# Hybrid decoder layer on one core: a written order for ScalarE and VectorE from the last head's output on, and a last row whose scaling is shared

## The chip, the cores and the metric

One Trainium2 chip, one core of it. The metric is the device time of one execution in microseconds (us); less is better. TensorE is called PE in the profile, VectorE DVE, ScalarE ACT, GpSimd POOL, and SyncE, which issues most transfers, SP.

## The reference

`x` is 1024 tokens by 1024 channels, float32, depth 1:

```python
h = rms_norm(x, norm_mix_g);  u = h @ w_in            # 1024 x 3328: pool 256 | q, f, i, g of 768 each
y_pool = pool_mixer(u_pool, pool_w, pool_scale)       # 4 groups of 64: trailing means over 2/4/8/16, minus the token, a 64x64 map
y_hgrn = hgrn2_mixer(q, f, i, g, lb, norm_g)          # 6 heads, state 128x128: S_t = f_t S_(t-1) + (1-f_t) i_t^T, o_t = S_t^T q_t,
                                                      # then o * rsqrt(mean(o^2)+eps) * norm_g * silu(g) for each head
x = x + concat(y_pool, y_hgrn) @ w_out
x = x + square(relu(rms_norm(x, norm_mlp_g) @ w_up)) @ w_down
return rms_norm(x, final_norm_g)
```

## The kernel before, in words

All products run in float32 made of two parts: `split` (L118 to L122) makes `hi`, a rounded copy by ACT (L121), and `lo`, the rest, by DVE (L122), and `mm3` (L124 to L129) makes one product of three matmuls, hi x hi, hi x lo, lo x hi (128x128 by 128x512 each). So every operand of a product passes through ACT first and DVE second.

The six recurrent heads come one after another. `hgrn(hd)` is a generator that stops before each of its stages ("near", "middle", "far", "keys", "updates", "output"), and between the stages the loop over heads draws steps of other work from `beside(hd)`: the projections of the next head, and beside the last head (hd = 5) the gate of head 4, the second pool input, and the gate of head 5. The table `LAGS` says how many steps are drawn ahead of each stage. In that loop the order of PE alone is written (`tc.manual_schedule(engines={PE})`); the instructions of ACT, DVE and POOL are placed by a scheduler, which may move an instruction ahead of others. Each engine then runs its own list strictly in that order.

Around the last head's output these matter:

- pool input 1 (`pool_input`, L550 on): u (L355), running sums `winK`, `winF` (L565, L566), two closing steps of 1.3 us (L572), then a split into `whi_win` and `wlo_win`, from which PE makes `psp` (`pool_output`), and ACT scales `psp` into `mix[1]` (L589).
- gate of head 5 (`gated`): for each half, ps_g times rms_row to g (L355, DVE), sigmoid of g into ps_g (L361, ACT), product into g (L362, DVE).
- stage "output" of head 5: PE makes `po` (L513, L515) in two banks; ACT squares each of its 8 blocks with a sum (L518); DVE makes the mean (L134, `ms_o`), POOL the power -1/2 (L136, `rstd_o`), DVE scales into `on` (L520). `mixed` transposes `on` on PE (`pto`, L542) and multiplies by the gate into the eighth block of the mixing output (L544).
- the output product: `w_out`'s left half is loaded in four pieces of two row blocks (`wo_1`, `wo_2`, `wo_3`, `wo_0`) into two raw buffers, so that the third load waits until the first piece is split; `mix_split(h, j)` splits block j of the mixing output into `mT`, half h of the tokens. PE takes the blocks in the order 2, 3, 4, 5, 6, 0, 1, 7. For the first two row tiles (`ps_o_0`, `ps_o_1`) it makes blocks 2, 3, 4, then `pto`, then the other five. After them come the row tiles from `ps_o_2` on.

At the very end (from L1134) the down projection's results are added to x row tile by row tile, each row's square sum is made by ACT (L1128), its mean by DVE (L1141), the power by POOL (L1143); the left 512 columns are scaled by DVE (L1147) and sent by SP (L1148), the right 512, already multiplied by the weight, are scaled by ACT (L1151) and sent from ACT's queue (L1152). The last row tile's last product is made in two pieces of 256 columns. Here DVE, ACT and POOL have a written order already.

Of the kernel before, what the change touches and what calls it, by code (L numbers as in the profile page):

```python
# [10 lines left out]
F32 = mybir.dt.float32  # L11
F32R = mybir.dt.float32r
# [20 lines left out]
STAGES = ("near", "middle", "far", "keys", "updates", "output")  # L33
LAGS = {48: (5, 14, 8, 4, 1, 9), 64: (6, 19, 10, 4, 1, 10), 96: (6, 19, 10, 5, 2, 14)}
LAGS = {steps: dict(zip(STAGES, lags)) for steps, lags in LAGS.items()}
# [30 lines left out]
def kernel(  # L66
# [116 lines left out]
    with ExitStack() as pa:  # L183
# [209 lines left out]
        def hgrn(hd, q, f, k, vt):  # L393
# [114 lines left out]
            on = ha.tile([P, NT, P], F32, tag="Kn", name=f"on_{hd}", bufs=1)  # L508
            for b in range(2):
                po = misc_ps(f"po_{hd}_{b}")  # L510
                for c in range(4):
                    i = 4 * b + c
                    pe.matmul(po[:, c * P:(c + 1) * P], sc[:, i, :], vt[:, i, :], start=True, stop=i == 0)  # L513
                    if i:
                        pe.matmul(po[:, c * P:(c + 1) * P], q[:, i * P:(i + 1) * P], st[:, i, :], start=False, stop=True)  # L515
                ss = small.tile([P, 4], F32, tag="sso", name=f"sso_{hd}_{b}")
                for c in range(4):
                    act.activation(junk[:, :P], po[:, c * P:(c + 1) * P], AF.Square, accum_out=ss[:, c:c + 1])  # L518
# [35 lines left out]
        def pool_input(kt, wins):  # L554
            u = ha.tile([P, S], F32, tag="GQ"[kt], name=f"u_{kt}", bufs=1 + kt)
            w = col_tile(kt * P, f"pool{kt}")

            ready_w["g"] = gate_weights(NH - 2 + kt)
# [17 lines left out]
            parts = [wring["split"][0].tile([P, S], F32R, tag=f"w{part}", name=f"w{part}_win_{kt}") for part in ("hi", "lo")]  # L576
# [163 lines left out]
        def row_block(src, r0, n, c0, name):  # L740
            return load_w(src[r0 * P:(r0 + n) * P, c0:c0 + 512].rearrange("(j p) c -> p j c", p=P), [n, 512], name)

        ws = [None] * (KT // 2)
        for j in MIX_ORDER[:-1:2]:
            ws[j // 2] = row_block(w_out[0], j // 2 * 2, 2, 0, f"wo_0_{j // 2}")
        mT = big_pair("mT")

        def mix_split(h, j):
            split(mT[h][0][:, j, :], mT[h][1][:, j, :], mix[j][:, h * 512:(h + 1) * 512])

        for pool_ in (psm, pss, psd):
            pool_.release()
        psb = ctx.enter_context(tc.tile_pool(name="psb", bufs=8, space=bass.MemoryType.PSUM, reuse_waits="tile"))

        def bank(name):
            return psb.tile([P, 512], F32, tag="bank", name=name)

        def products_out(banks, weight, js):

            for j in js:  # L760
                for i, ps in banks.items():
                    m, c = mT[i // 4], i % 4 * P
                    mm3(ps, (m[0][:, j, c:c + P], m[1][:, j, c:c + P]), weight(j), j == MIX_ORDER[0], j == MIX_ORDER[-1])

        def left_weight(j):
            hi, lo = ws[j // 2]
            return hi[:, j % 2, :], lo[:, j % 2, :]


        with tc.manual_schedule(engines={mybir.EngineType.PE}):  # L770
# [7 lines left out]
        for j in MIX_ORDER:  # L778
            mix_split(1, j)
# [338 lines left out]
    with ExitStack() as pd:  # L1118
# [30 lines left out]

        def right_rows(i, r):  # L1150
            act.mul(ys[i][:, 512:], ys[i][:, 512:], r)  # L1151
            act.dma_start(out[0, i * P:(i + 1) * P, 512:], ys[i][:, 512:])  # L1152
# [86 lines left out]
        with tc.manual_schedule(engines={mybir.EngineType.DVE, mybir.EngineType.Activation, mybir.EngineType.Pool}):  # L1239
# [3 lines left out]
            for (g, n), (pools, a, b) in zip(products[-2:], ((pools, a, b), ahead)):  # L1243
                for i, cs in product(g, n, a, b):
                    if cs.stop == 256:

                        ss = squares(i, cs)
                        left_rows(*ready)
# [3 lines left out]
                        continue  # L1252
                    ss = squares(i, cs)
                    if ready:
                        if cs.start % 512 == 0:
# [3 lines left out]
            left_rows(*ready)  # L1259
            right_rows(*ready)  # L1260
# [54 lines left out]
```

## Time and profile before

| | |
|---|---|
| time before, median of 3 runs | 1071.73 us (1071.65 to 1073.27) |
| the profiled execution's own time | 1071.58 us |
| its span, first to last instruction | 1069.8 us |
| PE busy | 1060.4 us (99%) |
| DVE busy | 741.7 us (69%) |
| ACT busy | 447.7 us (42%) |
| POOL busy | 77.3 us (7%) |
| granted clock of PE | 0.999 |

The time is 1.78 us more than the span, which lies around it. In a row of the timeline the first number is the start, the second the duration, both in us; "xN" merges N instructions of one form that follow each other; the bracket says how long the engine sat idle before, and on whom it waited. Instructions of one engine overlap a little, so that the next one starts some 0.06 to 0.1 us before the row of the one before it ends.

### The profile page before, as it was taken

What the parts mean: (1) busy time and instruction counts of PE and PEld (TensorE: products, weight loads), DVE (VectorE), ACT (ScalarE), POOL (GpSimd) and SP (SyncE); (2) the same over time, 40 slices, a digit from 0 to 9 for tenths busy, and PEclk for the clock granted to TensorE, in tenths of its full rate; (3) what the DMA queues carried; (4) which work ended last, traced back from release to release, by engine and by line L of the source; (5) the groups of instructions that cost most, each with busy time, mean ns of one, the idle gap of its engine ahead of it and who ended that gap; (6) DMA issues with size and microseconds to landing.
All of it is one profiled execution on the core that took longest, in us unless ns stands there. A gap on an engine that the chain in (4) does not pass through costs nothing.

```text
span 1069.8 us, 14595 instructions
## 1 busy us (share of the span) xinstructions
PE 1060.4 (99%) x5930; PEld 889.6 (83%) x5930; DVE 741.7 (69%) x928; ACT 447.7 (42%) x722; POOL 77.3 (7%) x126
## 2 busy tenths in 40 slices
PE   9999999999999999999999999999999999999997
PEld 8988889988888788888888888888888888888886
DVE  5377676166587924798856865876979878777775
ACT  5856545344444723463223223323435242423334
POOL 0001000001010111101101100100100000000001
PEclk9999999999999999999999999999999999999999
DMA  9521011031001633135435534428983344253104
GB/s 315 169 60 55 17 30 40 3 97 41 21 1 41 202 134 117 70 108 177 167 109 189 185 101 156 177 98 318 389 335 119 114 162 170 105 204 150 40 1 157
DMA packets 70515, 137.56 MB, mean 129 GB/s; under 512 B 5040, under 2 KB 44080, under 8 KB 66864
## 3 DMA queue, kind: packets, MB, share of 16 engines
q1 hardware_dynamic: 59808, 100.98, 27.8%
q0 software_dynamic: 9344, 33.56, 8.0%
q10 hardware_dynamic: 1296, 2.10, 0.5%
q8 instruction: 46, 0.75, 0.3%
q14 instruction: 21, 0.17, 0.1%
HBM read 98.87 MB, written 37.75 MB: 128 GB/s over the span
## 4 chain that ended last, share of the span: by engine, by line
PE 95%; DVE 3%; DMA 0%; issue 0%; POOL 0%; ACT 0%; SPq 0%; ACTq 0%; POOLq 0%
PE ps_ua L128 5%; PE ps_ua L127 5%; PE ps_ua L129 5%; PE ps_dx L129 5%; PE ps_dx L127 5%; PE ps_dx L128 5%; PE ps_v L283 3%; PE ps_dy L129 3%; PE ps_uc L128 3%; PE ps_dy L127 3%; PE ps_uc L127 3%; PE ps_uc L129 3%; PE ps_dy L128 3%; PE ps_o L129 2%; PE ps_o L128 2%; PE ps_o L127 2%
## 5 line engine op out<-in xcount | busy, mean ns | idle before, releaser
L121 ACT CAST wdop<-raw_wd 128x2048 fp32r<-128x2048 f32 x28 | 53.5, 1912 | 154.3 <-PE ps_dy L129 50.2
L127 PE MATMUL ps_ua<-h2op,whi_wu 128*128 128x512 f32 x256 | 99.7, 389 | 0.0
L129 PE MATMUL ps_ua<-h2op,wlo_wu 128*128 128x512 f32 x256 | 99.6, 389 | 0.0
L128 PE MATMUL ps_ua<-h2op,whi_wu 128*128 128x512 f32 x256 | 99.6, 389 | 0.0
L127 PE MATMUL ps_dx<-wdop,hop 128*128 128x512 f32 x252 | 98.0, 389 | 0.0
L128 PE MATMUL ps_dx<-wdop,hop 128*128 128x512 f32 x252 | 98.0, 389 | 0.0
L129 PE MATMUL ps_dx<-wdop,hop 128*128 128x512 f32 x252 | 98.0, 389 | 0.0
L122 DVE TENSOR_TENSOR wdop<-raw_wd,wdop 128x2048 fp32r<-128x2048 f32 x28 | 64.1, 2289 | 27.9 <-ACT wdop L121 27.9
L121 ACT CAST hop<-hraw 128x2048 fp32r<-128x2048 f32 x28 | 53.4, 1909 | 33.6 <-DMA hraw<-hid 21.0
L122 DVE TENSOR_TENSOR hop<-hraw,hop 128x2048 fp32r<-128x2048 f32 x28 | 63.9, 2283 | 2.2 <-ACT hop L121 2.2
L121 ACT CAST whi_wu<-wsum 128x1024 fp32r<-128x1024 f32 x22 | 23.2, 1053 | 93.6 <-DVE wsum L795 38.7
L122 DVE TENSOR_TENSOR wlo_wu<-raw_wu,whi_wu 128x1024 fp32r<-128x1024 f32 x23 | 28.0, 1221 | 47.6 <-ACT whi_wu L121 47.6
L798 DVE TENSOR_TENSOR x<-ps_dx,x 128x512 f32<-128x512 f32 x64 | 43.9, 687 | 18.7 <-PE ps_dx L129 18.7
L127 PEld LDWEIGHTS ps_ua<-h2op,whi_wu 128*128 128x128 f32 x256 | 48.1, 188 | 10.0
L129 PEld LDWEIGHTS ps_ua<-h2op,wlo_wu 128*128 128x128 f32 x256 | 48.0, 188 | 10.0
L128 PEld LDWEIGHTS ps_ua<-h2op,whi_wu 128*128 128x128 f32 x256 | 48.1, 188 | 9.9
L128 PEld LDWEIGHTS ps_dx<-wdop,hop 128*128 128x128 f32 x252 | 47.3, 188 | 9.9
L129 PEld LDWEIGHTS ps_dx<-wdop,hop 128*128 128x128 f32 x252 | 47.3, 188 | 9.8
L127 PEld LDWEIGHTS ps_dx<-wdop,hop 128*128 128x128 f32 x252 | 47.3, 188 | 9.8
L1031 POOL DMA_DIRECT2D hid<-hid x56 | 29.8, 532 | 283.6 <-DVE hid L1028 216.5
L127 PE MATMUL ps_uc<-h2op,whi_wu 128*128 128x512 f32 x128 | 49.8, 389 | 0.0
L128 PE MATMUL ps_uc<-h2op,whi_wu 128*128 128x512 f32 x128 | 49.8, 389 | 0.0
(280 smaller groups left out, 2706.4 us busy)
## 6 DMA issues: line engine op xcount, KB each, us to landing
hid<-hid POOLq DMA_DIRECT2D x56, 512.0 KB, 3.2
hraw<-hid SPq DMA_DIRECT2D x28, 1024.0 KB, 4.8
raw_wu<-in_w_up_dram SPq DMA_DIRECT2D x32, 512.0 KB, 3.8
raw_wd<-in_w_down_dram SPq DMA_DIRECT2D x16, 1024.0 KB, 7.1
xt<-in_x_t_dram SPq DMA_DIRECT2D x16, 256.0 KB, 5.4
xn<-in_x_dram SPq DMA_DIRECT2D x8, 512.0 KB, 7.9
x<-x_mid SPq DMA_DIRECT2D x8, 512.0 KB, 5.4
raw_q<-in_w_in_dram SPq DMA_DIRECT2D x6, 512.0 KB, 3.9
```

What stands on the lines that cost most here:

```text
L121: act.copy(hi, src)
L122: dve.tensor_tensor(out=lo, in0=src, in1=hi.bitcast(F32), op=ALU.subtract)
L127: pe.matmul(ps, lh, rh, start=start, stop=False, skip_group_check=goes_on)
L128: pe.matmul(ps, lh, rl, start=False, stop=False, skip_group_check=goes_on)
L129: pe.matmul(ps, ll, rh, start=False, stop=stop, skip_group_check=goes_on)
L283: pe.matmul(banks[i][:, :VC], hT[h][part][:, j, i * P:(i + 1) * P], w[:, b, :], start=j == 0 and part == 0 and w is wh, stop=j == KT - 1 a ...
L798: dve.tensor_tensor(out=out_, in0=a, in1=b, op=ALU.add)
L1031: nc.gpsimd.dma_start(store[n][:, at, :], t)
```

## The change

It has two parts.

At the last head: a stage "rows" is put into `hgrn` between the squares and the scaling of `on` (its lag is 0, so that nothing is drawn there). Once head 5 reaches "output", ACT and DVE follow the written order too, through the whole output product's first rows, which now stand within the same region as the loop over heads. In that order stand: the work beside the head, then both banks' squares and means; at "rows" the first piece of w_out (`wo_1`), the splits of blocks 2, 3, 4 and `wo_2`; then the scaling of `on`, the rest of the gate, and, by twos, `wo_3`, blocks 5 and 6, `wo_0`, blocks 0 and 1, `mixed`, block 7, and last the second half's splits. The two tiles of the pool windows' split are taken from their ring before the gate's weights. PE's order stays as it was.

At the end: of the last row tile all four parts of x are multiplied by the weight ahead (`weighted`), DVE makes the last square sum itself, and the scaling is cut at column 704: DVE the left 704, sent by SP, ACT the right 320, sent from ACT's queue (`last_rows`). The row tile before it is finished by ACT one step earlier.

```diff
@@ hgrn @@
             yield "output"
-            on = ha.tile([P, NT, P], F32, tag="Kn", name=f"on_{hd}", bufs=1)
+            pos = []
             for b in range(2):
...
                 for c in range(4):
                     act.activation(junk[:, :P], po[:, c * P:(c + 1) * P], AF.Square, accum_out=ss[:, c:c + 1])
-                r = rstd_of(ss, 4, P, small, f"o_{hd}_{b}")
+                pos.append((po, rstd_of(ss, 4, P, small, f"o_{hd}_{b}")))
+            yield "rows"
+            on = ha.tile([P, NT, P], F32, tag="Kn", name=f"on_{hd}", bufs=1)
+            for b, (po, r) in enumerate(pos):
                 dve.tensor_tensor(
@@ the loop over heads @@
-        with tc.manual_schedule(engines={mybir.EngineType.PE}):
+        def left_rows_of(j):
+            src = w_out[0][j * P:(j + 2) * P, :512].rearrange("(j p) c -> p j c", p=P)
+            ws[j // 2] = load_w(src, [2, 512], f"wo_0_{j // 2}")
...
+        with ExitStack() as in_order:
+            in_order.enter_context(tc.manual_schedule(engines={mybir.EngineType.PE}))
...
                 while stage:
+                    if hd == NH - 1 and stage == "output":
+                        in_order.enter_context(
+                            tc.manual_schedule(engines={mybir.EngineType.DVE, mybir.EngineType.Activation})
+                        )
...
+                    if hd == NH - 1 and stage == "rows":
+                        mix_operand(0)
+                        left_rows_of(MIX_ORDER[0])
+                        for j in MIX_ORDER[:3]:
+                            mix_split(0, j)
+                        left_rows_of(MIX_ORDER[2])
...
-            for j in MIX_ORDER[:-1]:
+            products_out(first_rows, left_weight, MIX_ORDER[:3])
+            left_rows_of(MIX_ORDER[4])
+            for j in MIX_ORDER[3:5]:
                 mix_split(0, j)
-            products_out(first_rows, left_weight, MIX_ORDER[:3])
+            left_rows_of(MIX_ORDER[5])
+            for j in MIX_ORDER[5:7]:
+                mix_split(0, j)
             mixed(NH - 1, on, gates[NH - 1], bank)
             mix_split(0, MIX_ORDER[-1])
             products_out(first_rows, left_weight, MIX_ORDER[3:])
@@ the end @@
+        def last_rows(i, r):
+            y, n = ys[i], 704
+            dve.tensor_scalar(y[:, :n], y[:, :n], r, None, op0=ALU.mult)
+            nc.sync.dma_start(out[0, i * P:(i + 1) * P, :n], y[:, :n])
+            act.mul(y[:, n:], y[:, n:], r)
+            act.dma_start(out[0, i * P:(i + 1) * P, n:], y[:, n:])
+
+        def weighted(i, cs):
+            dve.tensor_tensor(out=ys[i][:, cs], in0=xs[i][:, cs], in1=gf[:, cs], op=ALU.mult)
...
                         ss = squares(i, cs)
+                        weighted(i, cs)
                         left_rows(*ready)
...
+                    if cs.start == 256:
+                        ss = small.tile([P, 1], F32, tag="ss3", name=f"ss3_{i}_last", bufs=16)
+                        x_ = xs[i][:, cs]
+                        dve.scalar_tensor_tensor(
+                            out=junk[:, cs], in0=x_, scalar=1.0, in1=x_, op0=ALU.mult, op1=ALU.mult, accum_out=ss
+                        )
+                        r = row_scale(i, ss)
+                        weighted(i, cs)
+                        right_rows(*ready)
+                        last_rows(i, r)
+                        continue
...
-            left_rows(*ready)
-            right_rows(*ready)
```

ACT's list at the last head's output, before: `mT_hi` from mix_1227, mix_1675, mix_2286, mix_2750, mix_3206, mix_3170 are the casts of blocks 2, 3, 4, 5, 6 and 0, `po` and `sso` the squares, `whi_win` the cast of the pool windows, `ps_g` the gate's sigmoid, `wo` the pieces of w_out.

```order
L121 CAST mT_hi_3533<-mix_1227 128x512
L121 CAST mT_hi_3533<-mix_1675 128x512
L121 CAST mT_hi_3533<-mix_2286 128x512
L121 CAST mT_hi_3533<-mix_2750 128x512
L121 CAST mT_hi_3533<-mix_3206 128x512
L518 ACTIVATE junk,sso_0_3442<-po_0_3434 128x128
L121 CAST mT_hi_3533<-mix_3170 128x512
L121 CAST whi_win_3394<-winK_3066 128x512 x2
L361 ACTIVATE ps_g_0_3401<-g_3400 128x512
L518 ACTIVATE junk,sso_0_3442<-po_0_3434 128x128
L121 CAST whi_wo_1_3511<-raw_wo_1_3509 128x1024
L518 ACTIVATE junk,sso_0_3442<-po_0_3434 128x128
```

The same place on ACT after the change, from the pool windows' cast on, which now follows straight on the copies of `kn`:

```order
L121 CAST whi_win_3190<-winK_3066 128x512 x2
L361 ACTIVATE ps_g_0_3403<-g_3402 128x512
L518 ACTIVATE junk,sso_0_3443<-po_0_3435 128x128 x4
L518 ACTIVATE junk,sso_1_3461<-po_1_3452 128x128 x4
L121 CAST whi_wo_1_3474<-raw_wo_1_3472 128x1024
L121 CAST mT_hi_3470<-mix_1227 128x512
L121 CAST mT_hi_3470<-mix_1675 128x512
L121 CAST mT_hi_3470<-mix_2286 128x512
L121 CAST whi_wo_2_3486<-raw_wo_2_3484 128x1024
```

Six casts of `mT_hi` that stood ahead of the pool windows' cast now stand behind it, behind the sigmoid and behind all eight squares, which stand in one row.

DVE's list from the gate's first half on, before (`lo` parts of the same names; `ms_o`, `on` of head 5's output):

```order
L355 TENSOR_TENSOR g_3400<-ps_g_0_3401,rms_row 128x512
L122 TENSOR_TENSOR wlo_win_3395<-winK_3066,whi_win_3394 128x512 x2
L362 TENSOR_TENSOR g_3400<-ps_g_0_3401,g_3400 128x512
L122 TENSOR_TENSOR mT_lo_3534<-mix_1227,mT_hi_3533 128x512
L122 TENSOR_TENSOR wlo_wo_1_3512<-raw_wo_1_3509,whi_wo_1_3511 128x1024
L122 TENSOR_TENSOR wlo_wo_2_3518<-raw_wo_2_3515,whi_wo_2_3517 128x1024
L134 TENSOR_SCALAR ms_o_0_3447<-sso_0_3442 128x4
```

And after:

```order
L122 TENSOR_TENSOR wlo_win_3191<-winK_3066,whi_win_3190 128x512 x2
L355 TENSOR_TENSOR g_3402<-ps_g_0_3403,rms_row 128x512
L362 TENSOR_TENSOR g_3402<-ps_g_0_3403,g_3402 128x512
L134 TENSOR_SCALAR ms_o_0_3448<-sso_0_3443 128x4
L134 TENSOR_SCALAR ms_o_1_3466<-sso_1_3461 128x4
L122 TENSOR_TENSOR wlo_wo_1_3475<-raw_wo_1_3472,whi_wo_1_3474 128x1024
L122 TENSOR_TENSOR mT_lo_3471<-mix_1227,mT_hi_3470 128x512
L122 TENSOR_TENSOR mT_lo_3471<-mix_1675,mT_hi_3470 128x512
L122 TENSOR_TENSOR mT_lo_3471<-mix_2286,mT_hi_3470 128x512
L122 TENSOR_TENSOR wlo_wo_2_3487<-raw_wo_2_3484,whi_wo_2_3486 128x1024
L523 TENSOR_TENSOR on_3490<-po_0_3435,rstd_o_0_3450 128x512
L523 TENSOR_TENSOR on_3490<-po_1_3452,rstd_o_1_3468 128x512
```

The first lo part of w_out stands behind both means now, and the gate's first product behind the pool windows' lo part. Behind these rows DVE's list goes on with the gate's second half, `wo_3`, blocks 5 and 6, `wo_0`, blocks 0 and 1, where before the gate's second half stood among the scalings of `on`.

DVE's list at the very end, before and after (x_6409 is the last row tile, x_6407 the one before it):

```order
L798 TENSOR_TENSOR x_6409<-ps_last_8270,x_6409 128x256
L1147 SCALAR_TENSOR_TENSOR y<-x_6407,rstd_n_6_8268,gf 128x512
L1250 TENSOR_SCALAR ss_left<-ss_7_0_8284,ss_8092 128x1
L798 TENSOR_TENSOR x_6409<-ps_last_8290,x_6409 128x256
L1141 TENSOR_SCALAR ms_n_7_8308<-ss_7_256_8304,ss_left 128x1
L1147 SCALAR_TENSOR_TENSOR y<-x_6409,rstd_n_7_8310,gf 128x512
```

```order
L819 TENSOR_TENSOR x_6409<-ps_last_8270,x_6409 128x256
L1180 TENSOR_TENSOR y<-x_6409,gf 128x256
L1168 SCALAR_TENSOR_TENSOR y<-x_6407,rstd_n_6_8268,gf 128x512
L1283 TENSOR_SCALAR ss_left<-ss_7_0_8284,ss_8092 128x1
L819 TENSOR_TENSOR x_6409<-ps_last_8291,x_6409 128x256
L1290 SCALAR_TENSOR_TENSOR junk,ss_7_last<-x_6409 128x256
L1162 TENSOR_SCALAR ms_n_7_8307<-ss_7_last,ss_left 128x1
L1180 TENSOR_TENSOR y<-x_6409,gf 128x256
L1174 TENSOR_SCALAR y<-y,rstd_n_7_8309 128x704
```

Two multiplications by the weight and one square sum come to DVE; ACT loses that square sum.

More of the change, by code (lines that the diff above doesn't have):

```diff
@@ L30 @@
 FILL = 160
-STAGES = ("near", "middle", "far", "keys", "updates", "output")
+STAGES = ("near", "middle", "far", "keys", "updates", "output", "rows")
 LAGS = {48: (5, 14, 8, 4, 1, 9), 64: (6, 19, 10, 4, 1, 10), 96: (6, 19, 10, 5, 2, 14)}
-LAGS = {steps: dict(zip(STAGES, lags)) for steps, lags in LAGS.items()}
+LAGS = {steps: dict(zip(STAGES, (*lags, 0))) for steps, lags in LAGS.items()}
 FIRST_LAG = 9
@@ L556, in pool_input @@
             w = col_tile(kt * P, f"pool{kt}")
+            parts = [wring["split"][0].tile([P, S], F32R, tag=f"w{part}", name=f"w{part}_win_{kt}") for part in ("hi", "lo")]
             ready_w["g"] = gate_weights(NH - 2 + kt)
@@ L575, in pool_input @@
                 )
-            parts = [wring["split"][0].tile([P, S], F32R, tag=f"w{part}", name=f"w{part}_win_{kt}") for part in ("hi", "lo")]
             for h in range(2):
@@ L720, with mix_operand, mix_split @@
             split(*(w[pr, :, pr] for w in pws), pw[pr])
-        with tc.manual_schedule(engines={mybir.EngineType.PE}):
+        ws, mT = [None] * (KT // 2), []
+        def left_rows_of(j):
+            src = w_out[0][j * P:(j + 2) * P, :512].rearrange("(j p) c -> p j c", p=P)
+            ws[j // 2] = load_w(src, [2, 512], f"wo_0_{j // 2}")
+        def mix_operand(h):
+            mT.append(tuple(big.tile([P, KT, 512], F32R, tag="big", name=f"mT_{part}{h}") for part in ("hi", "lo")))
+        def mix_split(h, j):
+            split(mT[h][0][:, j, :], mT[h][1][:, j, :], mix[j][:, h * 512:(h + 1) * 512])
+        with ExitStack() as in_order:
+            in_order.enter_context(tc.manual_schedule(engines={mybir.EngineType.PE}))
             for hd in range(NH):
@@ L738 @@
                 finish(work)
[L740 to L767, printed above, removed]
@@ L770, with bank, products_out @@
-        with tc.manual_schedule(engines={mybir.EngineType.PE}):
+            for pool_ in (psm, pss, psd):
+                pool_.release()
+            psb = ctx.enter_context(tc.tile_pool(name="psb", bufs=8, space=bass.MemoryType.PSUM, reuse_waits="tile"))
+            def bank(name):
+                return psb.tile([P, 512], F32, tag="bank", name=name)
+            def products_out(banks, weight, js):
+                for j in js:
+                    for i, ps in banks.items():
+                        m, c = mT[i // 4], i % 4 * P
+                        mm3(ps, (m[0][:, j, c:c + P], m[1][:, j, c:c + P]), weight(j), j == MIX_ORDER[0], j == MIX_ORDER[-1])
@@ L771, with left_weight @@
+            def left_weight(j):
+                hi, lo = ws[j // 2]
+                return hi[:, j % 2, :], lo[:, j % 2, :]
             first_rows = {i: bank(f"ps_o_0_{i}") for i in range(2)}
-            for j in MIX_ORDER[:-1]:
+            products_out(first_rows, left_weight, MIX_ORDER[:3])
+            left_rows_of(MIX_ORDER[4])
+            for j in MIX_ORDER[3:5]:
                 mix_split(0, j)
-            products_out(first_rows, left_weight, MIX_ORDER[:3])
+            left_rows_of(MIX_ORDER[5])
@@ L777 @@
             products_out(first_rows, left_weight, MIX_ORDER[3:])
-        for j in MIX_ORDER:
-            mix_split(1, j)
+            mix_operand(1)
+            for j in MIX_ORDER:
+                mix_split(1, j)
     mixp.release()
@@ L1252 @@
                         continue
+                    if cs.start == 256:
[9 more added lines that the diff above has]
+                        continue
                     ss = squares(i, cs)
                     if ready:
-                        if cs.start % 512 == 0:
-                            left_rows(*ready)
+                        left_rows(*ready)
                         right_rows(*ready)
                     ready = i, row_scale(i, ss)
-            left_rows(*ready)
-            right_rows(*ready)
 _INS = [
```

## The prediction

> **What bounds the kernel now.** I read the page first, then PE's waits, then the timeline of ACT, DVE and PE around the last head's output, and last the end of the span.
>
> ```profile
> span 1069.8 us, 14595 instructions
> PE 1060.4 (99%) x5930; PEld 889.6 (83%) x5930; DVE 741.7 (69%) x928; ACT 447.7 (42%) x722; POOL 77.3 (7%) x126
> ```
>
> PE is busy for all but 9.4 us of the span, and most of those lie behind its last matmul. So a microsecond that PE loses anywhere is a microsecond of the time; nothing later can absorb it. The view of PE's waits has two rows:
>
> ```profile
> PE warm L230 <- DVE junk L228: 1.2, 1, 1.2
> PE ps_o L129 <- DVE mT_lo L122: 0.9, 2, 0.5
> ```
>
> The first is the opening. The second is all that the first part of the change can win: two waits, 0.9 us together, in the first rows of the output product. PE takes the first of those products, and is through with the two row tiles, here (the row at 369.48 is the first product of ps_o_2):
>
> ```profile
> 356.10 0.39 PE L127 MATMUL ps_o<-whi_wo,mT_hi 128*128 128x512 f32 x1
> ...
> 360.18 0.38 PE L542 MATMUL pto<-ident,on 128*128 128x128 f32 x2
> ...
> 369.25 0.39 PE L129 MATMUL ps_o<-whi_wo,mT_lo 128*128 128x512 f32 x1
> 369.48 0.40 PE L127 MATMUL ps_o<-whi_wo,mT_hi 128*128 128x512 f32 x1
> ```
>
> A product starts 0.23 us after the one before it. What PE finds ready at 356.10 depends on ACT and DVE in the ten microseconds before:
>
> ```profile
> 345.78 2.70 ACT L121 CAST mT_hi<-mix 128x512 fp32r<-128x512 f32 x5 [6.87 <-PE ps_g L128]
> ...
> 349.15 1.13 ACT L121 CAST whi_win<-winK 128x512 fp32r<-128x512 f32 x2
> 350.20 0.59 ACT L361 ACTIVATE ps_g<-g 128x512 f32<-128x512 f32 x1
> ```
>
> ```profile
> 347.63 1.28 DVE L572 SCALAR_TENSOR_TENSOR winK<-winF,pconst,u 64x1024 f32<-64x1024 f32 x1
> 348.95 0.35 DVE L504 SCALAR_TENSOR_TENSOR st<-st,dec,pu 128x128 f32<-128x128 f32 x1
> 349.21 0.69 DVE L355 TENSOR_TENSOR g<-ps_g,rms_row 128x512 f32<-128x512 f32 x1
> 349.81 1.28 DVE L122 TENSOR_TENSOR wlo_win<-winK,whi_win 128x512 fp32r<-128x512 f32 x2
> ...
> 352.21 2.36 DVE L122 TENSOR_TENSOR wlo_wo<-raw_wo,whi_wo 128x1024 fp32r<-128x1024 f32 x2
> ```
>
> ACT sat idle for 6.87 us, and the scheduler put five casts of `mT_hi` (2.70 us) there, while the pool windows were not yet done; both pieces of w_out were split by 354.6. That hoist hides what PE needs at 356.10.
>
> **The change part by part: the written order.** ACT now has the pool windows' cast directly behind the copies of `kn`. It waits there for the DVE step that starts at 347.63 in the row above. This step moves by two small edits of about 0.1 us each (one copy more behind `u`, an order of two steps); I take 347.8, end 349.1. Until then ACT stands still with the casts queued behind. From there the two lists give a chain in which each link waits for the one before:
>
> - Two casts of the windows (1.13): 349.1 to 350.25; the first half is there at 349.7, and DVE makes `wlo_win` (1.28) from 349.75 to 351.05. PE wants it at about 352 for `psp`, as before: no cost.
> - DVE now makes the gate's first product (0.69) only behind that, to 351.65, not in the gap at 349.21. The sigmoid (0.59) runs from 351.7 to 352.3.
> - Then the eight squares. Standing in a row they look as at an earlier head:
>
> ```profile
> 303.67 0.28 ACT L518 ACTIVATE junk<-po 128x128 bf16<-128x128 f32 x1
> 303.84 0.19 ACT L518 ACTIVATION_READ_ACCUMULATOR junk<-po 128x1 f32 x1
> 304.07 0.28 ACT L518 ACTIVATE junk<-po 128x128 bf16<-128x128 f32 x1
> ```
>
> - One square starts 0.40 after the one before it, so eight take 3.2 us: 352.2 to 355.4. Before, other work stood between them.
> - ACT casts `wo_1`, 1.05 by the row below: 355.4 to 356.5. Block 2's cast follows, 0.6 (five took 2.70): 357.0. DVE is held at the second mean until 355.5, then by `wo_1`'s cast. It makes `wlo_wo_1` from 356.53 to 357.7 and block 2's lo part to 358.3 (0.69).
>
> So PE's first product waits from 356.1 to 357.0, the second to 357.7, the third to 358.3: waits of 0.9, 0.5 and 0.4, 1.8 in all, where before there was none. From 356.53 DVE is the link without a gap: 1.13 for `wlo_wo_1` (two take 2.36), 3 x 0.60 for blocks 2, 3, 4 (five take 3.10 in the row below), 1.13 for `wlo_wo_2`, 2 x 0.60 for `on` and 0.69 for the gate's second half make 5.95: 362.5. The sigmoid (0.55) and the cast of `wo_3` (1.05 and handing over, 1.1) follow on ACT to 364.15, and DVE makes `wlo_wo_3` (1.13) and block 5's lo part (0.69): 365.97. The third product of block 5 waits for that.
>
> ```profile
> 357.28 1.05 ACT L121 CAST whi_wo<-raw_wo 128x1024 fp32r<-128x1024 f32 x1 [0.27 <-DMA raw_wo<-in_w_out_dram]
> ```
>
> ```profile
> 362.77 3.10 DVE L122 TENSOR_TENSOR mT_lo<-mix,mT_hi 128x512 fp32r<-128x512 f32 x5
> ```
>
> Block 5's products come on PE behind those of blocks 2, 3, 4 and `pto`. Its cast stands on ACT behind `wo_3`'s, which PE does not need before block 6: the written order makes block 5 wait for the wrong thing. PE, 18 products and the 1.0 us of `pto` behind its start, would be there at 363: it waits 1.6 for block 5's cast (364.6) and 0.9 for the lo part. Behind this wait it has 28 products up to ps_o_2 (1 and 3 of block 5, 6 each of blocks 6, 0, 1, 7): 28 x 0.23 = 6.44, from 366.03 to 372.47. Blocks 6, 0, 1 and 7 are ready at least 0.4 before PE wants them in this count. Before, ps_o_2 began at 369.48. **Loss: 3.0 us**, with the 0.9 of waits that disappear counted in. Its ends: 2.0 if a square costs no more than its own row, 0.28, since other work stood between them before; 3.5 if the windows come 0.3 later and a handing over costs 0.2 more.
>
> SP's transfers: `wo_3` may be fetched only once `wo_1`'s lo part is made, 357.7 now. The issue stood at 353.46 and the data at 357.28 (above), 3.8 later:
>
> ```profile
> 353.46 1.50 SPq L164 DMA_DIRECT2D raw_wo<-in_w_out_dram  x2
> ```
>
> So it lands at 361.5, wanted at 363.05: 1.5 to spare. `wo_0` is asked for at 360.7, lands at 364.5, and is wanted at 365.1: hidden, by 0.6. The loads of x and of w_up behind them in SP's queue go 3 us later too, as do their users. The other heads only get a few exchanged rows on DVE, where PE never waits. The second half's splits end near 376; PE wants them after two row tiles, 48 x 0.23 = 11 us behind 372.5.
>
> **The end.** All of it from 1062.64 on, but for SP:
>
> ```profile
> 1062.65 0.19 ACT L1128 ACTIVATION_READ_ACCUMULATOR junk<-x 128x1 f32 x1
> 1062.87 0.21 DVE L1250 TENSOR_SCALAR ss_left<-ss,ss 128x1 f32<-128x1 f32 x1
> ...
> 1063.00 0.41 DVE L798 TENSOR_TENSOR x<-ps_last,x 128x256 f32<-128x256 f32 x1
> 1063.51 0.42 ACT L1128 ACTIVATE junk<-x 128x256 bf16<-128x256 f32 x1 [0.67 <-DVE x L798]
> ...
> 1064.05 0.21 DVE L1141 TENSOR_SCALAR ms_n<-ss,ss_left 128x1 f32<-128x1 f32 x1 [0.64 <-ACT junk L1128]
> 1064.35 0.54 POOL L1143 TENSOR_TENSOR rstd_n<-ms_n,nhalf 128x1 f32<-128x1 f32 x1 [2.18 <-DVE ms_n L1141]
> ...
> 1064.92 0.75 DVE L1147 SCALAR_TENSOR_TENSOR y<-x,rstd_n,gf 128x512 f32<-128x512 f32 x1 [0.66 <-POOL rstd_n L1143]
> 1065.05 0.72 ACT L1151 ACTIVATE y<-y,rstd_n 128x512 f32<-128x512 f32 x1 [0.42 <-POOL rstd_n L1143]
> 1065.80 0.34 ACTq L1152 DMA_DIRECT2D out_dram<-y  x1
> ```
>
> The square sum on DVE: 256 columns take 0.41 with two tensors, and the form with a scalar 0.06 more (0.75 against 0.69): from 1063.45 to 1063.95, plus up to 0.19 if reading the sum out costs what it costs ACT. The mean starts between 1063.95 and 1064.15, where it was 1064.05: nothing to 0.1 won. The last scaling on ACT, 320 of 512 columns, lies between 0.42 (256) and 0.72 (512): 0.5, so 0.2 won. On DVE 704 columns in a form that the trace does not show: at TENSOR_TENSOR's rate (0.69 for 512, 0.53 more for 512 further) 0.89, 0.15 more than now; at the rate of the one copy with a single input,
>
> ```profile
> L302 DVE COPY rb<-rms_col 128x512 f32<-128x512 f32 x2 | 0.9, 428 | 2.4 <-POOL rms_col L300 2.4
> ```
>
> 0.43 for 512, some 0.55 for 704. I take 0.55, since this form too has one tensor going in. In the Trainium skill, "VectorE: DVE Perf Modes", section "The perf-mode tier table", says the same for fp32 from SBUF: twice the rate for tensor_scalar as for tensor_tensor; by its rule the sum stays as it is.
>
> Against this stands POOL. The two multiplications by the weight now run beside the powers of the last two row tiles, and at the last head such a neighbour (DVE's 0.69) went with a power of 1.31, the next one, without one for most of its time, took 1.01:
>
> ```profile
> 354.55 0.69 DVE L122 TENSOR_TENSOR mT_lo<-mix,mT_hi 128x512 fp32r<-128x512 f32 x1
> ```
>
> ```profile
> 354.79 1.31 POOL L136 TENSOR_TENSOR rstd_o<-ms_o,nhalf 128x4 f32<-128x4 f32 x1 [45.59 <-DVE ms_o L134]
> ...
> 357.65 1.01 POOL L136 TENSOR_TENSOR rstd_o<-ms_o,nhalf 128x4 f32<-128x4 f32 x1 [1.55 <-DVE ms_o L134]
> ```
>
> So 0 to 0.3 is lost, once or twice. The Trainium skill speaks against the change here: "GPSIMD Engine Reference", section "Specifications", has POOL share its SBUF interfaces with VectorE, with contention whenever a VectorE instruction has two SBUF inputs; by it the loss comes on both powers, 0.6 at most, and the end would be slower by 0.2 to 0.4. The sum by the rows: 0.25 won (0.05 at the mean, 0.2 at the scaling), less 0.15 for POOL, half of one such loss: **0.1 won**, between 0.5 won (no loss, the row tile before it sent earlier, out of the way) and 0.4 lost.
>
> **The sum.** The profiled execution took 1071.58, 0.15 under the median of 1071.73. 1071.58 + 3.0 - 0.1 = 1074.48, and for the median 1074.6. Its own range: 1071.73 + 2.0 - 0.5 = 1073.2 to 1071.73 + 3.5 + 0.4 = 1075.6.
>
> **The rivals.** *The order pays (not slower).* All of the chain hangs on the windows' cast. If DVE came to the windows' last step 3.0 earlier, at 344.8, the loss would be gone; at 343.9 PE waits nowhere, the 0.9 goes, 0.3 is won at the end, 1070.5. For it: two waits really go, ACT stands idle from 339, and DVE's steps of the windows have seven updates of the state between them (0.35 each) that a written order could have put behind. Against: the lists still have them there, but for the one exchange counted above. Chance 0.06.
>
> *Cheaper squares.* At 0.27 each ACT is 1.0 earlier and the whole chain with it: 1073.6. Chance 0.10.
>
> *A late load.* If `wo_3` or `wo_0` lands 2 us later than its 3.8, since it now meets other transfers, PE stands that much longer less the room of 0.6 to 1.5: about 1075.6. Chance 0.08.
>
> **How the numbers follow.** My forecast has 0.76. The range reaches from 1072.6 to 1076.2: both middle rivals and the forecast's own range, with 0.6 at each end for what the links' rows leave open; the rival on the other side is left out. About 0.2% (2.1 us) is what a measurement of this kernel can tell from no change, so the line for slower is 1073.87. From my forecast 0.04 falls under it, from the cheaper squares all 0.10, and the rival on the other side counts 0.04 as the same and 0.02 as faster. That makes 0.02 faster, 0.18 the same, 0.80 slower.
>
> **What would show it.** Right: ACT idle from the copies of `kn` to about 349.1, with no cast of `mT_hi` before the squares; eight squares 0.4 apart; PE waits at ps_o of 0.9, 0.5 and 0.4 for `mT_hi`, `wlo_wo` and `mT_lo`, and of 1.6 and 0.9 at block 5; ps_o_2 at 372.5; the last issue at 1068.7, which is 2.9 later than at present. Wrong: no waits of PE there beyond 0.9; or waits of this size and ps_o_2 earlier than 371.5.

## The result, and the profile after

| | before | after |
|---|---|---|
| median of 8 runs | 1071.68 us (1071.43 to 1073.27) | 1074.90 us (1074.04 to 1076.27) |
| ratio after/before, 95% interval | | 1.003 (1.0019 to 1.0041) |
| profiled execution, its span | 1071.58, 1069.8 us | 1074.86, 1073.0 us |

Slower by 0.3%, 3.2 us, where 2.9 were forecast. The busy times and the view of PE's waits:

```profile
PE 1061.4 (99%) x5930; PEld 889.6 (83%) x5930; DVE 743.3 (69%) x932; ACT 447.3 (42%) x720; POOL 76.6 (7%) x126
```

```profile
PE ps_o L127 <- ACT mT_hi L121: 2.2, 2, 1.5
PE warm L230 <- DVE junk L228: 1.2, 1, 1.2
PE ps_o L129 <- DVE mT_lo L122: 0.6, 1, 0.6
PE ps_o L128 <- DVE wlo_wo L122: 0.2, 1, 0.2
```

Busy times hardly move. The waits at ps_o, 0.9 before, are 3.0 now, and the first link is ACT. Its timeline shows why:

```profile
338.36 0.97 ACT L489 COPY kn<-ptk 128x512 f32<-128x512 f32 x2 [2.02 <-PE ptk L488]
349.68 1.14 ACT L121 CAST whi_win<-winK 128x512 fp32r<-128x512 f32 x2 [10.36 <-DVE winK L576]
352.26 0.60 ACT L361 ACTIVATE ps_g<-g 128x512 f32<-128x512 f32 x1 [1.44 <-DVE g L355]
...
353.18 0.28 ACT L518 ACTIVATE junk<-po 128x128 bf16<-128x128 f32 x1
...
353.58 0.28 ACT L518 ACTIVATE junk<-po 128x128 bf16<-128x128 f32 x1
...
355.84 1.04 ACT L121 CAST whi_wo<-raw_wo 128x1024 fp32r<-128x1024 f32 x1
356.78 1.66 ACT L121 CAST mT_hi<-mix 128x512 fp32r<-128x512 f32 x3
```

ACT stands idle for 10.36 us ahead of the windows' cast, and nothing that PE wants at 356 is made in that time. Squares start 0.40 apart; `whi_wo` and the first `mT_hi` follow behind them. PE in the same stretch, from the gate's last product to the first one of the third row tile:

```profile
356.31 0.39 PE L129 MATMUL ps_g<-hT_hi,wlo_g 128*128 128x512 f32 x1
357.45 0.51 PE L127 MATMUL ps_o<-whi_wo,mT_hi 128*128 128x512 f32 x1 [0.76 <-ACT mT_hi L121]
358.19 0.50 PE L128 MATMUL ps_o<-wlo_wo,mT_hi 128*128 128x512 f32 x1 [0.24 <-DVE wlo_wo L122]
358.80 0.50 PE L129 MATMUL ps_o<-whi_wo,mT_lo 128*128 128x512 f32 x1
...
362.56 1.03 PE L545 MATMUL pto<-ident,on 128*128 128x128 f32 x8
365.05 0.50 PE L127 MATMUL ps_o<-whi_wo,mT_hi 128*128 128x512 f32 x1 [1.46 <-ACT mT_hi L121]
...
366.39 0.50 PE L129 MATMUL ps_o<-whi_wo,mT_lo 128*128 128x512 f32 x1 [0.61 <-DVE mT_lo L122]
...
372.87 0.39 PE L127 MATMUL ps_o<-whi_wo,mT_hi 128*128 128x512 f32 x1
```

This execution's opening is later by 0.44 (the gate's last product started at 355.87 before), so I compare distances: from that product to the third row tile 372.87 - 356.31 = 16.56 now and 369.48 - 355.87 = 13.61 before (all starts). The stretch costs 2.95. This distance is the measure in all that follows, since it leaves out the opening and the end. In the idle brackets a wait looks smaller than it is, because a row behind a wait is drawn longer (0.50 for 0.39); from start to start the first two gaps are 1.14 and 0.74, less the usual 0.23.

The end, where the last add of x started at 1066.37:

```profile
1067.17 0.08 DVE L1290 DVE_READ_ACCUMULATOR junk<-x 128x1 f32 x1
1067.29 0.21 DVE L1162 TENSOR_SCALAR ms_n<-ss_last,ss_left 128x1 f32<-128x1 f32 x1
1067.42 0.41 DVE L1180 TENSOR_TENSOR y<-x,gf 128x256 f32<-128x256 f32 x1
1067.65 0.59 POOL L1164 TENSOR_TENSOR rstd_n<-ms_n,nhalf 128x1 f32<-128x1 f32 x1 [2.15 <-DVE ms_n L1162]
1068.27 0.59 DVE L1174 TENSOR_SCALAR y<-y,rstd_n 128x704 f32<-128x704 f32 x1 [0.43 <-POOL rstd_n L1164]
1068.86 0.37 ACTq L1177 DMA_DIRECT2D out_dram<-y  x1
1068.88 0.33 SPq L1175 DMA_DIRECT2D out_dram<-y  x1
```

From that add to the last issue it is 2.51 (1066.37 to 1068.88), before 2.80 (1063.00 to 1065.80): 0.29 won there. Counted from PE's last product it is 3.15 against 3.40, 0.25 won, since the add itself starts 0.04 later behind that product.

### The profile page after: what moved, and what is told of

The parts are those of the page before. It is cut to its first block, busy times and chain, and to the rows that moved or that the text cites. A ratio compares the mean times of both kernels' runs of the same rounds, so it can differ in the third digit from the quotient of the medians.

```text
span 1073.0 us, 14598 instructions
## 1 busy us (share of the span) xinstructions
PE 1061.4 (99%) x5930; PEld 889.6 (83%) x5930; DVE 743.3 (69%) x932; ACT 447.3 (42%) x720; POOL 76.6 (7%) x126
## 4 chain that ended last, share of the span: by engine, by line
PE 96%; DVE 2%; ACT 1%; DMA 0%; issue 0%; SPq 0%; POOLq 0%
PE ps_ua L129 5%; PE ps_ua L127 5%; PE ps_ua L128 5%; PE ps_dx L128 5%; PE ps_dx L127 5%; PE ps_dx L129 5%; PE ps_v L283 3%; PE ps_dy L128 3%; PE ps_uc L129 3%; PE ps_dy L127 3%; PE ps_uc L127 3%; PE ps_uc L128 3%; PE ps_dy L129 3%; PE ps_o L129 3%; PE ps_o L128 3%; PE ps_o L127 3%
```

## The experiments

My theory: the loss lies between the gate's last product and the third row tile, and its links are in this order the squares' end, the casts that stand behind it on ACT, DVE's lo parts, and piece 3's place ahead of block 5. The simple rival: the scheduler's hoist of the block casts is what was lost, and all of it. Other rivals: a late transfer, or a written order as such. The table gives what was measured; "distance" is the one above, from one profiled run of each kernel; "low" counts the runs whose mean granted clock over the whole execution was 0.996 or 0.997 (of all others, those of before included, it was 0.998 or 0.999).

| kernel | median us (runs) | ratio to before, 95% | low | distance |
|---|---|---|---|---|
| before | 1071.63 to 1071.68 (four sets) | | 0 | 13.61 |
| after | 1074.90 (8) | 1.0019 to 1.0041 | 2 | 16.56 |
| tail_only | 1071.80 (11) | 0.9992 to 1.0009 | 0 | not touched |
| order_only | 1076.12 (7) | 1.0023 to 1.0045 | 4 | 18.20, less 1.6 |
| squares_apart | 1073.66 (11) | 1.0013 to 1.0030 | 3 | 17.17, less 1.6 |
| block5_first | 1074.02 (11) | 1.0013 to 1.0031 | 0 | 16.06 |
| keep_busy | 1074.45 (9) | 1.0017 to 1.0037 | 0 | 16.57 |
| wo_casts_early | 1073.85 (9) | 1.0016 to 1.0035 | 3 | 15.80 |
| block_casts_early | 1075.12 (5) | 1.0021 to 1.0046 | 2 | 16.57 |
| both_hoists | 1074.33 (8) | 1.0018 to 1.0038 | 2 | 17.24, less 1.5 |
| casts_in_idle | 1070.50 (11) | 0.9980 to 0.9998 | 0 | 12.49 |
| last_row_halves | 1070.24 (11) | 0.9978 to 0.9996 | 0 | 12.49 |

"Less 1.6": in these three profiles PE's clock fell inside the stretch. From block 5's third product to the third row tile it is 6.48 in the profile after, and 8.10, 8.06 and 7.95 there; the difference is what the low clock took.

**tail_only**: the kernel before with the diff's second part, of which the calls are the core:

```diff
                         ss = squares(i, cs)
+                        weighted(i, cs)
                         left_rows(*ready)
...
+                        weighted(i, cs)
+                        right_rows(*ready)
+                        last_rows(i, r)
...
-            left_rows(*ready)
-            right_rows(*ready)
```

> The kernel before with the change's second part alone (the last row's scaling shared), everything up to the last row tile as before. My reading of the two traces: from the add of the last piece to the last issue 2.80 us became 2.51, so this is 0.3 faster than before, 1071.4, and POOL's two last powers stay at 0.54 to 0.60. Rival: the two multiplications by the weight slow the powers by 0.3 each, as the 1.31 beside a DVE row at the last head suggested; then this is 0.1 to 0.3 slower than before, 1071.9, and the powers show 0.8.

Measured: no difference that the times can show. The profile has the last issue 3.15 behind PE's last product, before 3.40, and POOL's powers at 0.54 and 0.59; so neither the gain of 0.3 in the time nor the rival's loss. In the profile the span ends 7.23 behind PE's last product, before 7.40: of the 0.25 won by the last issue 0.17 is left, too little for these times to show (see last_row_halves for what follows the issue).

**order_only**: the change with the same lines taken back.

```diff
-                        last_rows(i, r)
...
+            left_rows(*ready)
+            right_rows(*ready)
```

> The changed kernel with the end as it was before: the written order alone. If the loss is made between the last head's output and the third row tile and nowhere else, it is 3.0 (waits of PE of 0.8, 0.2, 0.3 at block 2 and 1.5, 0.6 at block 5), give or take 0.2: 1074.5 to 1074.9, 0.3 above what a sum with the end's 0.3 would leave for the whole change only if the two parts simply add. Rival: part of the 3.2 that was measured for the whole change comes from elsewhere (a lower granted clock behind the waits, a later opening); then this is 3.5 or more above before, 1075.2, with the third row tile still 3.0 later.

Measured: the runs split, three at 1074.44 to 1074.57 and four at 1076.12 to 1076.61, with nothing in between. The first group is what the loss of 3.0 gives. The profiled run is of the second, and its PE rows show what happens there, behind the two waits at block 5 (start, length):

```profile
366.24 0.39 PE L127 MATMUL ps_o<-whi_wo,mT_hi 128*128 128x512 f32 x1
...
367.32 0.63 PE L128 MATMUL ps_o<-wlo_wo,mT_hi 128*128 128x512 f32 x1
367.75 0.63 PE L129 MATMUL ps_o<-whi_wo,mT_lo 128*128 128x512 f32 x1
```

The view by windows, cut at the clock's own edges; the columns are the window, its length, PE's busy time, PE's granted clock, DMA share and GB/s:

```profile
363.53:366.94 3.41, 1.77 (x7) 1.00 0.68 185
366.94:370.35 3.41, 3.41 (x10) 0.51 0.75 230
```

For 3.4 us PE runs at half its clock; products start 0.43 apart instead of 0.23. It comes right behind a window of the same length in which PE was busy for 1.77 only. The Trainium skill, "TensorE: Matmul & The Clock Gate", section "What's actually happening", has a free-running window of some 3.4 us and half the clock after an idle one; length and half agree with these rows, but an idle window is not needed: one that was half busy was enough. So neither expectation covers it: the rival named a lower clock, but with the third row tile still 3.0 later, and here it is 18.20 - 13.61 = 4.59 later. Some runs pay a second loss, of 1.6 to 1.8, on top of the waits.

**squares_apart**, in `hgrn`, for the last head only:

```diff
-                    act.activation(junk[:, :P], po[:, c * P:(c + 1) * P], AF.Square, accum_out=ss[:, c:c + 1])
+                    act.activation(junk[:, c * P:(c + 1) * P] if hd == NH - 1 else junk[:, :P], po[:, c * P:(c + 1) * P], AF.Square, accum_out=ss[:, c:c + 1])
```

> The changed kernel in which the last head's four squares of a bank write four different stretches of the scratch tile, so that no square waits for the one before it; order and counts as they were. If the 0.40 between two squares is that wait, they come 0.27 to 0.28 apart, ACT is through 0.9 to 1.0 earlier, and since everything behind hangs on ACT and then on DVE in the written order, the third row tile starts 0.9 to 1.0 earlier and the time is 1.0 lower: 1073.9. If the 0.40 is what a square with a sum takes on ACT (0.28 and the reading of the sum), nothing moves: 1074.9. If the squares come closer and the time stays, then another wait (a transfer, the gate's product) binds and my chain is wrong.

Measured: the squares come 0.25 apart,

```profile
353.35 0.26 ACT L518 ACTIVATE junk<-po 128x128 bf16<-128x128 f32 x1
...
353.60 0.27 ACT L518 ACTIVATE junk<-po 128x128 bf16<-128x128 f32 x1
```

the wait for block 2's cast is gone, the distance is 15.6 (less the low clock) instead of 16.56, and the median is 1.24 lower. This profile's clock fell too. The 0.40 was a square's wait for the one before it, which wrote the same scratch columns, and my chain holds: what ACT saves, PE gains.

**block5_first**, after `products_out(first_rows, left_weight, MIX_ORDER[:3])`:

```diff
-            left_rows_of(MIX_ORDER[4])
             for j in MIX_ORDER[3:5]:
                 mix_split(0, j)
+            left_rows_of(MIX_ORDER[4])
```

> The changed kernel with blocks 5 and 6 split ahead of the third piece of w_out instead of behind it; nothing else is moved. By my chain PE waits at block 5 because its cast stands behind that of the piece (1.05 on ACT, 1.13 on DVE), which only block 6 needs: block 5's two waits (1.5 and 0.6) shrink by about 1.5 together, a new wait of about 1.0 appears at block 6 for the piece's lo part, and the time is 0.5 lower: 1074.4. If the order within this stretch does not matter (DVE has the same work to do before block 6), nothing is gained: 1074.9. If the piece's transfer is late, the wait at block 6 is 2 or more and the time rises.

Measured, PE's two waits behind `pto`:

```profile
364.08 0.50 PE L127 MATMUL ps_o<-whi_wo,mT_hi 128*128 128x512 f32 x1 [0.51 <-ACT mT_hi L121]
366.81 0.50 PE L128 MATMUL ps_o<-wlo_wo,mT_hi 128*128 128x512 f32 x1 [0.52 <-DVE wlo_wo L122]
```

As expected: block 5 waits 1.5 less, block 6 waits for the piece's lo part, and 0.50 of distance is won. None of 11 runs shows the low clock. The median is 0.88 lower, more than the 0.5 expected; that two of the eight runs of after had the low clock explains a part of that, the rest is open.

**keep_busy**, ahead of block 5 in PE's list:

```diff
             mixed(NH - 1, on, gates[NH - 1], bank)
+            fill = bank("fill")
+            for _ in range(5):
+                pe.matmul(fill, junk[:, :P], junk, start=True, stop=True)
```

> The changed kernel with five extra products of the zeroed scratch tile on PE (0.23 each) between the transposes of the last head's output and block 5, where PE otherwise stands idle for 1.5 us; their result is not used. In the written order alone, one profiled run showed a granted clock of 0.50 for 3.4 us right behind the two waits at block 5, eight products at 0.43 instead of 0.23, 1.6 us on top of the waits; other runs of the same kernel show none of it. If PE's idle time in the 3.4 us before is what brings the lower clock, it is gone here: all runs with a mean clock of 0.998 or more, none above 1075.3, and a median of 1074.5 to 1074.7, since the five products fit in the wait. If the clock falls for another reason (a stretch of the program, the chip), a third of the runs still show 0.996 and 1075.5 to 1076.5. If the five products get in the way, all runs are slower by up to 1.2.

Measured: the distance is the same, no run of 9 has the low mean clock, seven lie at 1074.16 to 1074.89. Two are at 1076.01 and 1076.17, which I had not expected; the second is the profiled one, and its loss lies elsewhere, in the opening: its gate's last product starts at 357.64, 1.33 later than after. In PE's row for 6 to 8 us (first this kernel, then after) 7 products stand where there were 12:

```profile
6.00:8.00 2.00, 2.00 (x7) 1.00 1.03 382
```

```profile
6.00:8.00 2.00, 2.00 (x12) 1.00 1.01 362
```

So PE was slow there for longer, which the clock column, 1.00 in both, does not show; whether it has the same cause stays open. Counting all runs: 16 of 48 are low in the six kernels that wait 2 us or more in all at block 5, none of 53 in the five that do not, none of 70 of before. (The mean misses some: both_hoists' profiled run has 0.998, and its clock fell.) keep_busy changes nothing but PE's idleness there. With the low clock in a third of the runs, 0 of 9 would come by chance about once in forty times ((2/3)^9 = 0.026), and block5_first adds 0 of 11; so that the idle time brings the low clock is well supported, though two runs above 1075.3 are not what the expectation said. How much idle time it takes can be narrowed by the windows of 3.41 us with the least PE work between 354 and 373, taken in steps of 0.2 us. In the six kernels PE is busy there for 1.1 to 1.4 us, in block5_first and keep_busy for 2.29 (here keep_busy):

```profile
356.80:360.21 3.41, 2.29 (x9) 1.00 0.00 0
```

A window with 1.77 was enough in order_only, and 0 of 20 runs fell where none has less than 2.29; so, as an estimate, the limit lies somewhere between these two, if the profile's busy time is what counts. One such window alone does not bring the fall: in the profile after the clock stayed up behind one with 1.34.

```profile
363.00:366.41 3.41, 1.34 (x9) 1.00 0.79 244
366.41:369.82 3.41, 3.41 (x15) 1.00 0.64 197
```

What decides which runs are hit, no run here shows.

**wo_casts_early**: where the region is entered, ACT's half alone of the split of both pieces; DVE's half stays at "rows".

```diff
+                        rows_hi(MIX_ORDER[0])
+                        rows_hi(MIX_ORDER[2])
```

> The changed kernel in which ACT casts the first two pieces of w_out (1.05 each) before its idle stretch ahead of the pool windows' cast, instead of behind the squares; the lo parts stay where they are on DVE. By my chain the squares' end then frees block 2's cast at once, DVE makes the first lo part of w_out 0.8 to 1.0 earlier, everything behind goes with it, and the time is 0.8 to 1.0 lower: 1073.9 to 1074.1 (with no drop of the clock). If the loss comes from the casts of the blocks that the scheduler had hoisted, and not from w_out, this brings nothing: 1074.9.

Measured: distance 15.80, 0.76 won, median 1.05 lower. The prediction's chain again, a little less than I gave it.

**block_casts_early**: the windows' split is put off until PE has the products of the gate's first half, and ahead of it stand the casts (`mix_hi`, ACT's half of a block's split); `mix_lo`, DVE's half of `mix_split`, takes its place for blocks 2 to 6.

```diff
+        def hoisted():
+            mix_operand(0)
+            for j in MIX_ORDER[:5]:
+                mix_hi(0, j)
```

> The changed kernel in which the casts of blocks 2 to 6 stand again where the scheduler had put them, in ACT's idle stretch ahead of the pool windows' cast; w_out's casts and all of DVE's order stay as in the changed kernel. The simple theory says that this hoist is what the written order lost, so that the 3.0 come back: 1071.9. My chain says that it brings nothing, 0 to 0.2: block 2 then waits for the first piece of w_out, whose cast still stands behind the squares, and block 5's third product still waits for its lo part, which stands on DVE behind the third piece's; only the first products of blocks 2 and 5 start earlier. PE's waits at block 5 become a single one of 2.2 to 2.5, so that the lower clock shows in as many runs as before or more: 1074.6 in runs without it, 1076 to 1076.5 in runs with it.

Measured: nothing, 16.57 against 16.56. PE's waits only change their names:

```profile
PE ps_o L129 <- DVE mT_lo L753: 2.3, 1, 2.3
...
PE ps_o L128 <- DVE wlo_wo L122: 0.8, 1, 0.8
PE ps_o L127 <- ACT whi_wo L121: 0.3, 1, 0.3
```

The hoist that the order visibly took away is, by itself, worth nothing.

**both_hoists**: the two edits together.

> The changed kernel with both sets of casts in ACT's idle stretch at once (blocks 2 to 6, and the first two pieces of w_out), everything else as written: DVE's order, the squares, the third piece ahead of blocks 5 and 6. Either set alone left the other as the next link, so their separate results (0.8 and 0.0 by the distance from the gate's last product to the third row tile) do not say what both bring. If the lost hoist is the whole loss, both bring the 3.0 back and that distance is that of before, 13.6 against 16.6. By my chain DVE's written order is the next link: the first lo part of w_out stands behind both means (the squares' end), and block 5's lo part behind the third piece's, whose cast ACT makes only behind the sigmoid that waits for DVE's second product of the gate. Then 0.8 to 1.0 come back, the distance is 15.6 to 15.8, one wait of about 2 us stays at block 5's third product, with a lower clock in a third of the runs or more.

Measured: 17.24, less 1.5 of low clock: 15.8, no better than wo_casts_early alone. One wait of 2.3 for block 5's lo part stays. On DVE the first lo part of w_out starts only behind the second mean,

```profile
355.20 0.17 DVE L134 TENSOR_SCALAR ms_o<-sso 128x4 f32<-128x4 f32 x1 [1.44 <-ACT junk L518]
355.28 1.22 DVE L763 TENSOR_TENSOR wlo_wo<-raw_wo,whi_wo 128x1024 fp32r<-128x1024 f32 x1
```

so the simple rival falls: with these hoists back on ACT, 2.2 of the 2.95 are still lost. The rows put them with what stands ahead of DVE's lo parts: the squares and means, and, at block 5, piece 3; what each of these takes with the hoists in place was not measured apart.

**casts_in_idle**: both hoists and squares_apart; `gated` takes a callback between sigmoid and product, which makes the lo parts of pieces 1 and 0 there; at "output" the lo parts of piece 2 and block 2 stand ahead of the squares' means; blocks 5 and 6 ahead of piece 3, and the gate's last products drawn before them. PE's order is unchanged.

```diff
             act.activation(ps, sl, AF.Sigmoid)
+            between()
             dve.tensor_tensor(out=sl, in0=ps, in1=sl, op=ALU.mult)
```

> The changed kernel with both hoists and what my chain says must go with them: casts of blocks 2 to 6 and of the first two pieces of w_out in ACT's idle stretch, squares that do not wait for each other, the lo parts of w_out's pieces 1 and 0 on DVE in the gaps while the gate's sigmoids run, pieces 3 and 0 asked for as soon as the lo parts of pieces 1 and 2 are made, blocks 5 and 6 ahead of piece 3. PE's order is unchanged. By my chain PE then waits nowhere in the first rows of the output product, not even the 0.9 of before, so the third row tile starts 0.9 before that of before and 3.9 before that of the change: 1070.5 to 1070.9, faster than both. If a written order as such is the loss (the scheduler's knowledge of the loads, say), waits of 1 us or more remain, for a transfer, and the time is 1072 or more.

Measured: 1070.50, faster than the change by 4.4 and than before by 1.2; the interval against before, 0.9980 to 0.9998, only just leaves out no difference. The distance, 12.49, is 1.12 shorter than that of before, where 0.9 was expected. PE's waits, then ACT (the first piece of w_out, and the stretch ahead of the windows' cast), then PE:

```profile
PE warm L230 <- DVE junk L228: 1.2, 1, 1.2
PE ps_v L283 <- DVE wlo_v L122: 0.2, 1, 0.2
```

```profile
326.15 1.05 ACT L760 CAST whi_wo<-raw_wo 128x1024 fp32r<-128x1024 f32 x1 [1.35 <-DMA raw_wo<-in_w_out_dram]
...
345.33 2.70 ACT L751 CAST mT_hi<-mix 128x512 fp32r<-128x512 f32 x5 [6.87 <-PE ps_g L128]
348.87 1.14 ACT L121 CAST whi_win<-winK 128x512 fp32r<-128x512 f32 x2 [0.84 <-DVE winK L577]
```

```profile
355.43 0.39 PE L129 MATMUL ps_g<-hT_hi,wlo_g 128*128 128x512 f32 x1
355.65 0.39 PE L127 MATMUL ps_o<-whi_wo,mT_hi 128*128 128x512 f32 x1
...
367.92 0.39 PE L127 MATMUL ps_o<-whi_wo,mT_hi 128*128 128x512 f32 x1
```

No wait is left at ps_o, so a written order as such is not what costs the time. The windows' cast comes as late as in the change (6.56 ahead of the gate's last product, there 6.63) and still waits for DVE: the prediction's first rival, in which that cast had to come 3.0 earlier, was not the only way to win. This run moves all the links at once and does not say which of them were needed.

**last_row_halves**: casts_in_idle with `y, n = ys[i], 512`.

> The kernel with the casts in the idle stretch, but the last row's scaling cut at column 512 instead of 704 (DVE 512, ACT 512). The traces so far say that the new end issues its last transfers 0.27 earlier than before, and that the span then ends 4.10 to 4.27 behind the last issue, where it was 3.97 to 4.00: 352 and 160 KB land after 2.6 and 2.8, 256 and 256 KB after 2.0. If it is the unequal cut, the end here comes 4.0 behind the last issue, and the last issue 0.15 later, for ACT's 512 columns take 0.72 instead of 0.56: nothing won or lost, 1070.5. If it is that both transfers start at the same moment, the end still comes 4.1 to 4.2 behind and the kernel is 0.15 slower, 1070.6 to 1070.7. The time alone cannot tell these apart; the profile's distances can.

Measured: 1070.24, 0.26 lower than casts_in_idle, which these intervals do not tell apart. In the profiles it is 7.40 from PE's last product to the span's end before, 7.27 after, 7.34 in casts_in_idle, 7.10 here. The span ends 3.80 behind the last issue (1068.3 - 1064.50), where 4.0 or 4.1 to 4.2 were expected. The "256 and 256 KB after 2.0" from which both started is the median of four rows of output; the last two transfers alone are these, before, after and here (KB, us from issue to landing):

```profile
out_dram<-y SPq DMA_DIRECT2D x1, 256.0 KB, 2.1
out_dram<-y ACTq DMA_DIRECT2D x1, 256.0 KB, 2.8
```

```profile
out_dram<-y SPq DMA_DIRECT2D x1, 352.0 KB, 2.6
out_dram<-y ACTq DMA_DIRECT2D x1, 160.0 KB, 2.8
```

```profile
out_dram<-y SPq DMA_DIRECT2D x1, 256.0 KB, 2.1
out_dram<-y ACTq DMA_DIRECT2D x1, 256.0 KB, 2.5
```

So the unequal cut is not shown to be what lands late: with the equal cut of before the last transfer took 2.8 as well. From the first of the two issues to the last landing it is 2.9 before (1065.7 to 1068.6), 2.8 after (1068.86 to 1071.66) and 2.7 here (1064.26 to 1067.00), nearly the same for 512 KB however they are cut. This run also moved the issues apart, 0.24 here (1064.26 and 1064.50) against 0.02 after, so whether the cut or the spacing made the 0.24 between casts_in_idle and this kernel (7.34 - 7.10) stays open.

## Why the prediction was right

- *The chain's head.* The windows' last step was to start at 347.8 and started at 348.36, which is 347.92 with the opening's 0.44 taken off. The windows' cast came at 349.24 by the same count, forecast 349.1.
- *The squares.* 0.40 apart, as the rows of the earlier head said; squares_apart shows the cause, which the prediction did not name. The rival of cheaper squares was not what the change did.
- *PE's waits.* Forecast 0.9, 0.5, 0.4 at block 2; from start to start 0.91, 0.51, 0.38 (each gap less 0.23). At block 5 forecast 1.6 and 0.9. There block 5 started 2.49 behind `pto`, 0.79 in casts_in_idle without a wait: 1.70; its third product came 1.34 behind its first, 0.55 there: 0.79.
- *The third row tile.* Forecast 372.47, measured 372.87, or 372.43 less the opening. Loss forecast 3.0, measured 2.95.
- *The loads.* No cast of `wo_3` or `wo_0` waited for its data in the profile after: the late load didn't come, and in casts_in_idle, which asks for them earlier, they were waited for on ACT (0.56 and 1.30) without a wait on PE.
- *The end.* Forecast 0.1 won; 7.40 - 7.27 = 0.13, in one execution of each, while tail_only's times show nothing. That the two agree is luck. Up to the last issue the prediction had 0.25 won less 0.15 for POOL, 0.10 in all; measured 0.25 in all, with 0.05 instead of 0.15 lost at POOL (the last power took 0.59 against 0.54) and so 0.30 won besides. What the sum put at nothing is what follows the issue: the last landing comes 2.8 behind it before and after, but the span ends 1.2 behind that landing before and 1.3 after, and no run shows why. The contention of POOL with VectorE that the Trainium skill names ("GPSIMD Engine Reference", section "Specifications"), to which I had given up to 0.6, is not borne out at that size. Beside the last power the multiplication ran for 0.18 (1067.65 to 1067.83); the power of the row before took 0.54, as without a neighbour, though the other multiplication ran beside it for 0.26 (the power from 1064.96, the multiplication from 1065.24). So even the 0.05 is not shown to be contention. One reading in the prediction was off: its own bounds for the mean, 1063.95 to 1064.15 against 1064.05, run from 0.1 won to 0.1 lost, and not from nothing to 0.1 won. Measured, the mean came 0.13 earlier behind the add (0.92 against 1.05).
- *The sum.* 1071.58 + 2.95 - 0.13 = 1074.40 against 1074.86 in the profiled run: the opening's 0.44 is the rest. The median lies 0.3 above my 1074.6, with two of its eight runs at a low clock, 1075.75 and 1076.27; without these two it is 1074.76, so the low clock makes about half of that difference. That term is missing from my sum: behind waits of this size I priced only the waits. In order_only it made the median 1.6 worse.

Where the prediction's prose was loose: it said "the written order makes block 5 wait for the wrong thing", as one cause among equals. The runs give its size, 0.5 of the 3.0, and that of each other link: the squares' mutual wait 1.0, w_out's casts 0.8, the blocks' casts 0. They do not add, since each frees only up to the next link.

## What to carry to other kernels

An order that is written by hand has to be written for each engine's idle stretches: ask of each operand of the next PE product where both of its halves, ACT's and DVE's, stand, since a hoist of one link of a chain can be worth nothing while the other is late (the blocks' casts alone: 0). Waits of PE can cost more than their length: here, where PE was busy for 1.8 us or less of some 3.4, a third of the runs had half the clock behind it and paid some 1.5 us besides, and none had it once the waits were split or filled. Look at the clock by windows when runs of one kernel form two groups. Read the landing of the last transfers from their own rows: a median over all rows of output hid that the last one took 2.8 and not 2.0.

## What was not expected of the hardware

- Half clock for 3.4 us after 1.64 us of idle time (3.41 - 1.77) in the 3.4 us before (order_only); 1.5 to 1.6 us lost each time in the three profiles, in a third of the runs of kernels with such waits. The opening varies as well, by 1.3 us in keep_busy's profile, while the clock column stays at 1.00.
- DVE reads out a square sum in 0.08, ACT in 0.19 to 0.20; the mean starts 0.92 behind the add (1066.37 to 1067.29), before 1.05.
- TENSOR_SCALAR takes 0.59 for 704 columns, 0.55 being forecast from a copy's row, and 0.49 for 512 (last_row_halves).
